# Two transformer blocks in one launch: another order of work between block 1's experts and block 2's attention

## The chip, the cores and the metric

The kernel runs on one core of a Trainium2 chip. The metric is device time in microseconds (us): the time of the program from start to end on that core, as the median of several runs. Five engines work side by side, each through its own list of instructions, in the order in which they stand in that list: TensorE (PE in the profile, its weight loads PEld), VectorE (DVE), ScalarE (ACT), GpSimd (POOL) and SyncE (SP, which here only starts transfers). An instruction that waits for another engine holds up everything behind it on its own engine.

## The reference

Two blocks run one after the other on 256 tokens of width 1024. Block 1 is attention with convolution, and then a mixture of 32 experts; block 2 is a gated pooling and attention block with a feed-forward layer. What matters here is the seam between them:

```python
# end of block 1
h = h + rms_norm(ffn, post_ffn_norm)          # ffn: routed experts + shared expert
# start of block 2
u = rms_norm_2(h, norm_mix)
proj = u @ w_in                                # pooling, q, k, v and two gates
z_pool, q, k, v, g_pool, g_attn = jnp.split(proj, splits, axis=-1)
y_pool = multiscale_pool(z_pool, w_pool_group, pool_scale) @ w_pool_branch
y_attn = windowed_gqa(q, k, v, sink) @ w_attn_branch
merged = jax.nn.sigmoid(g_pool) * y_pool + jax.nn.sigmoid(g_attn) * y_attn
h = h + merged @ w_out
```

`multiscale_pool` takes, for each of four groups of 128 channels, a centred mean over 2, 4, 8 or 16 tokens minus the token, and multiplies it by a 128x128 matrix of its group. `windowed_gqa` is attention with 8 query heads over 2 key heads.

## The kernel before

The 256 tokens are two tiles of 128, tile 0 and tile 1. Each fp32 operand of a large product is split in a high part (rounded to the type that TensorE takes at full rate) and a low part (the rest): ScalarE casts the high part, VectorE subtracts to get the low one. A product is then three matmuls, high by high, high by low, low by high (`mm3`, lines 278, 279 and 280). Weights stream in through `W`: SyncE starts the loads, `W.take()` hands out the next granule, `W.ahead()` splits granules in advance (lines 122 and 125).

The work around the change stands in this order in the code:

1. The experts' results are brought back to token order by one-hot matmuls (`scatter`, line 1143) and the shared expert is added (`shared_last`, line 1136), into PSUM tiles `ffn[i][n]`, i the token tile, n the half of 512 columns. Tile 1's part of it is spread around tile 0's next steps.
2. `residual(i, ...)` closes block 1 for tile i: ScalarE squares the two halves of `ffn[i]` (line 204), VectorE multiplies them by the gain into `mg` (`gained`, line 319), works out the inverse root in eight short instructions (lines 247, 222, 224 and 251; the profile shows three of them merged), adds to the residual stream `h` (line 251) and multiplies by the next gain (line 338). For the second half of a tile in `late` the gain product comes after the first half's line 338.
3. `half_T` (line 258) transposes four 128x128 blocks of `mg` into a PSUM tile `tr`. From it `split` (lines 76 and 77) writes the high part `uTh` on ScalarE and the low part `uTl` on VectorE.
4. `u_cols("q2", i, ...)` makes the queries of tile i: eight steps k of three matmuls, 24 in all, into the PSUM tile `q`. Steps 0 to 3 read the first half of `uTh` and `uTl`, steps 4 to 7 the second half.
5. Then come the keys and values (`kv`), and four times `pool_in(g)` (24 matmuls into `zp`, then sums over tokens on VectorE that end in `res`) and `pool_group(g, res)` (line 1379, a matmul of `res` into `pg`, an instruction on VectorE at line 1381, a split). Between them stand `scores2(i, j)` (line 1322: two PSUM tiles `s2a` and `s2b`, which VectorE reads at line 251 into `pr`) and `softmax2(i)`.

A scheduler sets the order on each engine. It takes the order of the code as the base and `tc.issue_after(x)` as an added condition that an instruction stands behind x. PSUM tiles come from two pools of four buffers each: `mm` (`tr`, `q`, `kv`, `zp`, `gt`, and `ffn[1]`) and `acc` (`s2a`, `s2b`, `pg`, `q2T`, `pT2`, `av2`). A pool hands its buffers out in turn, and a tile can be written only when the readers of the last tile in its buffer are done.

Of the kernel before, what the change touches and what calls it, by code (L numbers as in the profile page):

```python
# [11 lines left out]
F32 = mybir.dt.float32  # L12
# [8 lines left out]
P = 128  # L21
# [39 lines left out]
def block_kernel(ctx, tc, rwt, x, meta, pos, wst, gains, cst, pvec, rbias, sink, wpg, cst2, out):  # L61
    nc = tc.nc
    PE, ACT, DVE, POOL = nc.tensor, nc.scalar, nc.vector, nc.gpsimd
# [153 lines left out]
    last = [None] * 3  # L217
# [35 lines left out]
    def half_T(src, b, p=P):  # L253

        pt = mmt("tr")
        v = pt[:, :4 * p].rearrange("q (a t) -> q a t", a=4)
        for a in range(4):
            PE.transpose(v[:, a], src[:, (4 * b + a) * P:(4 * b + a + 1) * P], ident[:p, :p])
        return v

    def transpose_split(src, hi, lo, p, c0, n=8, pts=None):

        for b, v in enumerate(pts or [half_T(src, b, p) for b in range(n // 4)]):
            ins = split(v, hi[:, 4 * b:4 * b + 4, c0:c0 + p], lo[:, 4 * b:4 * b + 4, c0:c0 + p])
        return ins
# [57 lines left out]
    def residual(i, parts, g, g_next, s2, c=None, c32=1 / 32, late=(0,)):  # L323


        s = sm(2)
        mg = w4("mg")
        for n, a in enumerate(parts):
            sl = slice(n * 512, n * 512 + 512)
            last[0] = square(a, s[:, n:n + 1], c32)  # L330
            if n == 0 or i not in late:
                gained(mg[:, sl], a, c, g[:, sl])
        r = rstd(s)
        for n in range(2):
            sl = slice(n * 512, n * 512 + 512)
            with tc.issue_after(ins.ins) if n else nullcontext():
                stt(h[:, i, sl], mg[:, sl], r, h[:, i, sl], ALU.mult, ALU.add)
            last[1] = ins = DVE.tensor_mul(mg[:, sl], h[:, i, sl], g_next[:, sl])
            if i in late and n == 0:
                with tc.issue_after(ins.ins):  # L340
                    gained(mg[:, 512:], parts[1], c, g[:, 512:])
        return mg
# [33 lines left out]
    with tc.tile_pool(name="p1", bufs=1) as p1:  # L376
# [465 lines left out]
        ws = [W.take() for _ in range(4)]  # L842
# [4 lines left out]
        s2 = sm(4)  # L847
# [4 lines left out]
        nx = []  # L852
# [12 lines left out]
    with tc.tile_pool(name="p2", bufs=1) as p2:  # L865
# [76 lines left out]
        for c in (0, S):  # L942
            for i in range(2):
                oh_ins = DVE.tensor_scalar(oh[:, i, c:c + S], cs[:, C_IOTA + c:C_IOTA + c + S], code[:, i:i + 1],
                                           None, op0=ALU.is_equal)
# [11 lines left out]
        ws = [W.take() for _ in range(4)]  # L957
# [171 lines left out]
        ffn = [[acct("ffn00"), acct("ffn01")], None]  # L1129
# [9 lines left out]
        def scatter(i, gs):  # L1139
            for g in gs:  # L1140
                for n in range(2):
                    for a in range(2):
                        PE.matmul(ffn[i][n], sel[:, g, i * P:(i + 1) * P],
                                  ys[g][:, a * D + n * 512:a * D + (n + 1) * 512], start=False,
                                  stop=g == 3 and a == 1, skip_group_check=True)

        g_pf = gain("post_ffn")
        g_m2 = gain("mix2")
# [67 lines left out]
                        DVE.tensor_copy(raw, pa)  # L1216
                        DVE.tensor_add(ffn[i][n], ffn[i][n], raw)
        s2 = sm(4)
        nx = [residual(0, ffn[0], g_pf, g_m2, s2)]
        scatter(1, (0, 2))  # L1220
        shared_last(1, (1,))
        W.drop(WHOLE[2])
        pts = [half_T(nx[0], 0)]
        scatter(1, (1,))
        pts.append(half_T(nx[0], 1))
        scatter(1, (3,))
    pg.close()


    with tc.tile_pool(name="p3", bufs=1) as p3:  # L1230
        uTh = p3.tile([P, 8, S], F32R, name="uTh", tag="th")
        uTl = p3.tile([P, 8, S], F32R, name="uTl", tag="tl")
        with tc.tile_pool(name="p3a", bufs=1) as q3:
# [22 lines left out]

            rn, dgs = [], []

            def u_cols(name, i, ws, n):

                o = mmt(name)[:, :n]
                c = G // n
                for k in range(8):
                    w = ws[k // c]
                    mm3(o, [(uTh[:, k, i * P:(i + 1) * P], uTl[:, k, i * P:(i + 1) * P],
                             kb(w[0], k % c, n), kb(w[1], k % c, n))], k == 0, k == 7)
                return o
# [15 lines left out]
                ACT.copy(kT[:, i * P:(i + 1) * P], o)  # L1283

            o_q = []
            transpose_split(nx[0], uTh, uTl, P, 0, pts=pts)
            ws = [W.take() for _ in range(4)]
            o_q.append(u_cols("q2", 0, ws, 512))
            nx.append(residual(1, ffn[1], g_pf, g_m2, s2))
            with tc.issue_after(last[0].ins):  # L1290
                h_squares(0, s2)
            rn.append(rstd(s2[:, 0:2]))
# [11 lines left out]
            ws = [W.take() for _ in range(2)]  # L1304
# [13 lines left out]
            def scores2(i, j):  # L1318
                o = [acct("s2a"), acct("s2b")]
                for a in range(2):  # L1320
                    for b in range(2):
                        PE.matmul(o[b][:, a * S:(a + 1) * S],
                                  qT[b * 64:(b + 1) * 64, j + a, i * P:(i + 1) * P],
                                  kT[b * 64:(b + 1) * 64], start=True, stop=True, skip_group_check=True)
                for b in range(2):
                    for a in range(2):
                        hd = b * 4 + j + a
                        stt(pr[i][:, hd], c2[:, 64 + i * 256:320 + i * 256], 2.0 ** -(hd + 1),
                            o[b][:, a * S:(a + 1) * S], ALU.mult, ALU.add)
                    DVE.tensor_reduce(mxs[i][:, b * 4 + j:b * 4 + j + 2], pr[i][:, b * 4 + j:b * 4 + j + 2],  # L1330
                                      axis=AX.X, op=ALU.max)

            def softmax2(i):
                mx = mxs[i]
                DVE.tensor_tensor(mx, mx, skb, op=ALU.max)
                nm = sm(8)
                DVE.tensor_scalar(nm, mx, -1.0, None, op0=ALU.mult)
                es = sm(8)
                DVE.tensor_tensor(es, skb, nm, op=ALU.add)
                ACT.activation(es, es, AF.Exp)  # L1340
                for hd in range(NH):
                    ACT.activation(pr[i][:, hd], pr[i][:, hd], AF.Exp, bias=nm[:, hd:hd + 1],
                                   accum_out=sus[i][:, hd:hd + 1])
                return es
# [32 lines left out]
            def pool_group(g, res):  # L1377
                o = acct("pg")[:, :S]
                PE.matmul(o, kb(wpt, g), res, start=True, stop=True)
                y = pw("yp")[:, :S]  # L1380
                DVE.tensor_scalar(y, o, pv_[:, V_PSC + g:V_PSC + g + 1], None, op0=ALU.mult)
                split(y, yph[:, g], ypl[:, g])
# [61 lines left out]
            res = [pool_in(0)]  # L1444
            scores2(0, 0)
            scores2(0, 2)
            es0 = softmax2(0)
            pool_group(0, res[0])
            res.append(pool_in(1))
            scores2(1, 0)  # L1450
            scores2(1, 2)
            es1 = softmax2(1)
            pool_group(1, res[1])
            res.append(pool_in(2))
            denom(0, es0)
            pTx = [q3.tile([P, 2, 512], F32, name="pTa", **kw) for kw in ({}, {"tag": "q4"})]
            pTb = [[t[:, c] for t in pTx for c in range(2)], 0]
# [40 lines left out]
            ws = [W.take() for _ in range(4)]  # L1498
            s2 = sm(4)
            out_last(o2, gh, gl, ws, 0)  # L1500
            W.ahead(1)
            nx = [normed(0, o2[0], g_f2, s2)]
# [11 lines left out]
        with tc.tile_pool(name="p3b", bufs=1) as q3:  # L1514
# [55 lines left out]
            ws = [W.take() for _ in range(4)]  # L1570
# [25 lines left out]
            ws = [W.take() for _ in range(4)]  # L1596
            for d in range(4):
                down(18 + d, ws[d], 0)
            s2 = sm(4)
# [194 lines left out]
```

## Time and profile before

| | |
|---|---|
| median of 3 runs | 789.06 us (788.62 to 791.53) |
| the profiled execution: its own time | 790.79 us |
| the profiled execution: span from first to last instruction | 788.8 us |
| TensorE busy | 766.5 us, 97% of the span |
| VectorE busy | 611.8 us, 78% |
| ScalarE busy | 468.7 us, 59% |
| mean granted TensorE clock | 0.992 of full speed |

The profile is one execution. Its times below are counted from the start of the span. Busy TensorE is a model for the ends of matmuls, so starts are read rather than ends. The place of the change lies at about 440 to 500 us.

### The profile page before, as it was taken

Reading aid. Unit: us, or ns where it says so; the run is one execution under the profiler, and the core shown is the slowest. Engines: PE = TensorE matmul, PEld = TensorE weight load, DVE = VectorE, ACT = ScalarE, POOL = GpSimd, SP = SyncE. Lnnn points to the kernel's source line nnn. Section 1 sums busy time; section 2 is a strip of 40 time slices with the busy share of each in tenths; the row PEclk is TensorE's granted clock in tenths of the full one; section 3 lists DMA queues with packets and bytes.
Section 4 is the critical chain, followed back from the end, with each engine's and each line's share of the span. In section 5 each row is a group of like instructions: output and inputs, shape, how many; then the busy total and the mean of one; then the engine's idle time right before and its main releaser. Section 6 shows DMA issues by size and latency. Waiting matters only on the chain. (4 is left out here: it accounts for less than half of the span.)

```text
span 788.8 us, 11966 instructions
## 1 busy us (share of the span) xinstructions
PE 766.5 (97%) x4579; PEld 665.4 (84%) x4579; DVE 611.8 (78%) x987; ACT 468.7 (59%) x697; POOL 45.7 (6%) x62
## 2 busy tenths in 40 slices
PE   7989999999999999999999899999999999999996
PEld 5979985788888888888877688999988999999995
DVE  5878678799999989998988879766868566566565
ACT  5656445488887878887776466434555444444442
POOL 5641200000000000000000100000000000000000
PEclk9989999999999999999999999999999999999999
DMA  8737354589898979998998751444445545555101
GB/s 338 306 108 248 108 214 160 215 332 369 317 359 317 371 287 370 370 369 312 371 355 307 262 186 56 161 160 163 165 163 208 199 173 197 178 188 186 54 1 54
DMA packets 27212, 182.48 MB, mean 231 GB/s; under 512 B 3328, under 2 KB 3584, under 8 KB 6160
## 3 DMA queue, kind: packets, MB, share of 16 engines
q1 hardware_dynamic: 25344, 176.96, 60.5%
q0 software_dynamic: 1056, 3.71, 1.4%
q10 hardware_dynamic: 752, 1.01, 0.4%
q8 instruction: 37, 0.61, 0.3%
q14 instruction: 23, 0.19, 0.1%
HBM read 180.62 MB, written 1.05 MB: 230 GB/s over the span
## 5 line engine op out<-in xcount | busy, mean ns | idle before, releaser
L125 DVE TENSOR_TENSOR wlo<-raw,whi 128x1024 fp32r<-128x1024 f32 x324 | 391.4, 1225 | 84.7 <-ACT whi L122 77.5
L122 ACT CAST whi<-raw 128x1024 fp32r<-128x1024 f32 x326 | 337.6, 1049 | 176.0 <-PE gu L279 49.1
L278 PE MATMUL gu<-whi,xg 128*128 128x512 f32 x256 | 102.8, 401 | 0.0
L279 PE MATMUL gu<-wlo,xg 128*128 128x512 f32 x256 | 101.3, 396 | 0.0
L280 PE MATMUL gu<-whi,xg 128*128 128x512 f32 x256 | 100.6, 393 | 0.0
L279 PE MATMUL gu<-u2l,whi 128*128 128x256 f32 x320 | 90.6, 283 | 0.0
L278 PE MATMUL gu<-u2h,whi 128*128 128x256 f32 x320 | 90.6, 283 | 0.0
L280 PE MATMUL gu<-u2h,wlo 128*128 128x256 f32 x320 | 90.5, 283 | 0.0
L279 PEld LDWEIGHTS gu<-u2l,whi 128*128 128x128 f32 x320 | 61.5, 192 | 0.0
L280 PEld LDWEIGHTS gu<-u2h,wlo 128*128 128x128 f32 x320 | 61.4, 192 | 0.0
L278 PEld LDWEIGHTS gu<-u2h,whi 128*128 128x128 f32 x320 | 61.4, 192 | 0.0
L279 PEld LDWEIGHTS gu<-wlo,xg 128*128 128x128 f32 x256 | 48.2, 188 | 11.1 <-DVE wlo L125 1.4
L280 PEld LDWEIGHTS gu<-whi,xg 128*128 128x128 f32 x256 | 48.1, 188 | 10.5
L278 PEld LDWEIGHTS gu<-whi,xg 128*128 128x128 f32 x256 | 48.1, 188 | 9.9
L280 PE MATMUL y<-whi,hl 128*128 128x512 f32 x128 | 50.5, 394 | 0.0
L279 PE MATMUL y<-wlo,hh 128*128 128x512 f32 x128 | 50.5, 394 | 0.0
L278 PE MATMUL y<-whi,hh 128*128 128x512 f32 x128 | 49.1, 400 | 0.0
L278 PE MATMUL f<-whi,sh 128*128 128x512 f32 (+1 forms) x110 | 38.2, 349 | 0.0
L279 PE MATMUL f<-wlo,sh 128*128 128x512 f32 (+1 forms) x110 | 38.1, 349 | 0.0
L280 PE MATMUL f<-whi,sl 128*128 128x512 f32 (+1 forms) x110 | 37.7, 347 | 0.0
L278 PE MATMUL gt<-uTh,whi 128*128 128x256 f32 x128 | 36.7, 287 | 0.0
L280 PE MATMUL gt<-uTh,wlo 128*128 128x256 f32 x128 | 36.3, 283 | 0.0
(457 smaller groups left out, 1480.8 us busy)
## 6 DMA issues: line engine op xcount, KB each, us to landing
raw<-in_wst_dram SPq DMA_DIRECT2D x164, 1024.0 KB, 4.8
gain<-in_gains_dram POOLq DMA_DIRECT2D x6, 512.0 KB, 4.4
raw<-in_wst_dram SPq DMA_DIRECT2D x5, 512.0 KB, 8.1
h<-in_x_dram SPq DMA_DIRECT2D x2, 512.0 KB, 4.8
cs<-in_cst_dram SPq DMA_DIRECT2D x1, 612.0 KB, 16.6
out_dram<-mg ACTq DMA_DIRECT2D x2, 256.0 KB, 2.8
out_dram<-mg SPq DMA_DIRECT2D x2, 256.0 KB, 2.6
c<-in_cst_dram POOLq DMA_DIRECT2D x1, 288.0 KB, 3.1
```

The lines of the kernel that those rows point to most:

```text
L122: ACT.copy(hi, src)
L125: eng.tensor_sub(lo, src, hi.bitcast(F32))
L278: PE.matmul(o, sh, mh, start=first and i == 0, stop=False, skip_group_check=True)
L279: PE.matmul(o, sh, ml, start=False, stop=False, skip_group_check=True)
L280: last_mm[0] = PE.matmul(o, sl, mh, start=False, stop=last and i == n - 1, skip_group_check=True)
```

## The change

Four things are changed in the code. First, in `residual(0, ...)` no half is late: both gain products of tile 0 stand ahead of the inverse root. Second, the low half of tile 0's first four transposed blocks must stand behind the last product of that residual (`mul_ins`), and the last four blocks are no longer transposed ahead of the queries but between steps 3 and 4 of tile 0's query product, with their split there. Third, `residual(1, ...)` stands behind the second high half of tile 0 (`hi_ins`), and both its halves are late. Fourth, `pool_group(0)` moves behind the scores of tile 1, and `pool_group(1)` behind `pool_in(2)`.

```diff
--- before.py
+++ after.py
@@ -1216,14 +1216,13 @@
                         DVE.tensor_copy(raw, pa)
                         DVE.tensor_add(ffn[i][n], ffn[i][n], raw)
         s2 = sm(4)
-        nx = [residual(0, ffn[0], g_pf, g_m2, s2)]
+        nx = [residual(0, ffn[0], g_pf, g_m2, s2, late=())]
+        mul_ins = last[1]
         scatter(1, (0, 2))
         shared_last(1, (1,))
         W.drop(WHOLE[2])
         pts = [half_T(nx[0], 0)]
-        scatter(1, (1,))
-        pts.append(half_T(nx[0], 1))
-        scatter(1, (3,))
+        scatter(1, (1, 3))
     pg.close()
 
 
@@ -1256,11 +1255,13 @@
 
             rn, dgs = [], []
 
-            def u_cols(name, i, ws, n):
+            def u_cols(name, i, ws, n, done=None):
 
                 o = mmt(name)[:, :n]
                 c = G // n
                 for k in range(8):
+                    if done:
+                        done(k)
                     w = ws[k // c]
                     mm3(o, [(uTh[:, k, i * P:(i + 1) * P], uTl[:, k, i * P:(i + 1) * P],
                              kb(w[0], k % c, n), kb(w[1], k % c, n))], k == 0, k == 7)
@@ -1283,10 +1284,19 @@
                 ACT.copy(kT[:, i * P:(i + 1) * P], o)
 
             o_q = []
-            transpose_split(nx[0], uTh, uTl, P, 0, pts=pts)
+            def first_cols(k):
+
+                if k % 4 == 0:
+                    v = pts[0] if k == 0 else half_T(nx[0], 1)
+                    hi_ins[0] = ACT.copy(uTh[:, k:k + 4, :P], v)
+                    with tc.issue_after(mul_ins.ins):
+                        DVE.tensor_sub(uTl[:, k:k + 4, :P], v, uTh[:, k:k + 4, :P].bitcast(F32))
+
+            hi_ins = [None]
             ws = [W.take() for _ in range(4)]
-            o_q.append(u_cols("q2", 0, ws, 512))
-            nx.append(residual(1, ffn[1], g_pf, g_m2, s2))
+            o_q.append(u_cols("q2", 0, ws, 512, first_cols))
+            with tc.issue_after(hi_ins[0].ins):
+                nx.append(residual(1, ffn[1], g_pf, g_m2, s2, late=(0, 1)))
             with tc.issue_after(last[0].ins):
                 h_squares(0, s2)
             rn.append(rstd(s2[:, 0:2]))
@@ -1445,13 +1455,13 @@
             scores2(0, 0)
             scores2(0, 2)
             es0 = softmax2(0)
-            pool_group(0, res[0])
             res.append(pool_in(1))
             scores2(1, 0)
             scores2(1, 2)
+            pool_group(0, res[0])
             es1 = softmax2(1)
+            res.append(pool_in(2))
             pool_group(1, res[1])
-            res.append(pool_in(2))
             denom(0, es0)
             pTx = [q3.tile([P, 2, 512], F32, name="pTa", **kw) for kw in ({}, {"tag": "q4"})]
             pTb = [[t[:, c] for t in pTx for c in range(2)], 0]
```

What this makes of each engine's list is shown at three places. The first is TensorE where the experts' scatter ends and the queries of block 2 begin (`ffn_4318` is the second half of tile 1, `tr` a PSUM tile of transposed blocks, `q` the query tile of token tile 0). Before:

```order
L1143 MATMUL ffn_4318<-yg_4319,sel 128x512
L258 MATMUL tr<-ident,mg 128x128 x4
L1143 MATMUL ffn_4318<-yg_4319,sel 128x512
L258 MATMUL tr<-ident,mg 128x128 x4
L278 MATMUL q_4566<-whi,uTh 128x512
```

After:

```order
L1143 MATMUL ffn_4318<-yg_4319,sel 128x512 x2
L258 MATMUL tr<-ident,mg 128x128 x4
L278 MATMUL q_4557<-whi,uTh 128x512
L279 MATMUL q_4557<-wlo,uTh 128x512
L280 MATMUL q_4557<-whi,uTl 128x512
```

The second four transposes have left this place: they stand behind the twelfth query matmul now, and twelve more follow them.

The second place is VectorE's list behind the inverse root of tile 0 (`ffn_4317` and `ffn_4318` are the two halves of tile 1, `sm` a short instruction of tile 1's inverse root). Before:

```order
L251 SCALAR_TENSOR_TENSOR h<-mg,sm_4505,h 128x512
L77 TENSOR_TENSOR uTl<-tr,uTh 128x4x128
L338 TENSOR_TENSOR mg<-h,gain 128x512
L319 TENSOR_TENSOR mg<-ffn_4317,gain 128x512
L319 TENSOR_TENSOR mg<-ffn_4318,gain 128x512
L77 TENSOR_TENSOR uTl<-tr,uTh 128x4x128
L247 SCALAR_TENSOR_TENSOR sm_4599<-sm_4591 128x1
```

After:

```order
L251 SCALAR_TENSOR_TENSOR h<-mg,sm_4506,h 128x512
L338 TENSOR_TENSOR mg<-h,gain 128x512
L1293 TENSOR_TENSOR uTl<-tr,uTh 128x4x128 x2
L319 TENSOR_TENSOR mg<-ffn_4317,gain 128x512
L247 SCALAR_TENSOR_TENSOR sm_4598<-sm_4591 128x1
```

Tile 0's last product (line 338) stands ahead of both low halves now, and everything of tile 1's residual stands behind the second low half. The gain product of `ffn_4318` has moved further back, behind tile 1's first line 338.

The third place is TensorE at the scores of tile 1 and the first pooling product (`zp_4914` and `zp_4908` are the pooling input of group 1, `zp_4997` of group 2; `res_4861` is the result of group 0). Before, the product stood among the matmuls of group 1:

```order
L278 MATMUL zp_4914<-uTh_4547,whi_4716 128x256
L279 MATMUL zp_4914<-uTl_4548,whi_4716 128x256
L1379 MATMUL pg_4905<-res_4861,wpt_4556 128x256
L280 MATMUL zp_4914<-uTh_4547,wlo_4717 128x256
L278 MATMUL zp_4914<-uTh_4547,whi_4716 128x256
```

After, it stands among those of group 2, behind the scores of tile 1:

```order
L1332 MATMUL s2a_4962<-kT2_4553,qT2_4555 128x256
L1332 MATMUL s2b_4963<-kT2_4553,qT2_4555 128x256
L278 MATMUL zp_4997<-uTh_4542,whi_4742 128x256
L279 MATMUL zp_4997<-uTl_4543,whi_4742 128x256
L280 MATMUL zp_4997<-uTh_4542,wlo_4743 128x256
L278 MATMUL zp_4997<-uTh_4542,whi_4742 128x256
L279 MATMUL zp_4997<-uTl_4543,whi_4742 128x256
L1389 MATMUL pg_4974<-res_4861,wpt_4551 128x256
```

The scores of tile 1 now follow those of tile 0 with 24 matmuls and no pooling product between them, so their four PSUM tiles take the four `acc` buffers that the scores of tile 0 held, in the same turn, and `pg_4974` takes the next one. The second pooling product has moved by 19 matmuls behind the first, to the end of group 2.

## Rows read from the trace of the kernel before

**Rows 1.** Waits of TensorE, 436 to 530 us: total us, times, longest us.

```profile
PE tr L258 <- DVE mg L338: 1.9, 1, 1.9
PE pg L1379 <- DVE res L1374: 1.8, 2, 1.3
```

**Rows 2.** Timeline of TensorE: start, us, instruction, idle before and its releaser.

```profile
445.19 0.60 PE L258 MATMUL tr<-ident,mg 128*128 128x128 f32 x4
...
447.88 0.63 PE L258 MATMUL tr<-ident,mg 128*128 128x128 f32 x4 [1.85 <-DVE mg L338]
448.26 0.48 PE L278 MATMUL q<-whi,uTh 128*128 128x512 f32 x1
...
453.82 1.04 PE L258 MATMUL tr<-ident,mg 128*128 128x128 f32 x8
455.20 0.49 PE L373 MATMUL rs<-dg,ones 128*128 128x128 f32 x2 [0.34 <-DVE dg L367]
455.44 0.48 PE L278 MATMUL q<-whi,uTh 128*128 128x512 f32 x1
```

**Rows 3.** Timeline of VectorE at the two residuals.

```profile
443.03 0.69 DVE L338 TENSOR_TENSOR mg<-h,gain 128x512 f32<-128x512 f32 x1
443.64 0.68 DVE L319 TENSOR_TENSOR mg<-ffn,gain 128x512 f32<-128x512 f32 x1
444.36 0.75 DVE L251 SCALAR_TENSOR_TENSOR h<-mg,sm,h 128x512 f32<-128x512 f32 x1
446.44 0.69 DVE L77 TENSOR_TENSOR uTl<-tr,uTh 128x512 fp32r<-128x512 f32 x1 [1.33 <-ACT uTh L76]
447.05 0.68 DVE L338 TENSOR_TENSOR mg<-h,gain 128x512 f32<-128x512 f32 x1
...
449.77 0.15 DVE L247 SCALAR_TENSOR_TENSOR sm<-sm 128x1 f32<-128x1 f32 x1
...
451.23 0.75 DVE L251 SCALAR_TENSOR_TENSOR h<-mg,sm,h 128x512 f32<-128x512 f32 x1
...
452.02 0.69 DVE L338 TENSOR_TENSOR mg<-h,gain 128x512 f32<-128x512 f32 x1
```

**Rows 4.** Timeline of ScalarE at tile 0's first high half.

```profile
445.82 0.59 ACT L76 CAST uTh<-tr 128x512 fp32r<-128x512 f32 x1
446.31 0.60 ACT L204 ACTIVATE junk<-ffn 128x512 bf16<-128x512 f32 x1
...
447.03 0.63 ACT L204 ACTIVATE junk<-h 128x512 bf16<-128x512 f32 x1
```

**Rows 5.** Timeline of TensorE at the pooling products and the scores of tile 1.

```profile
475.11 0.70 PE L1379 MATMUL pg<-res,wpt 128*128 128x256 f32 x2 [1.28 <-DVE res L1374]
475.46 0.47 PE L280 MATMUL zp<-uTh,wlo 128*128 128x256 f32 x1
...
478.37 0.48 PE L1322 MATMUL s2a<-kT,qT 64*128 64x256 f32 x1
...
480.33 0.38 PE L278 MATMUL zp<-uTh,whi 128*128 128x256 f32 x1
...
484.09 0.70 PE L1379 MATMUL pg<-res,wpt 128*128 128x256 f32 x2 [0.51 <-DVE res L1374]
```

**Rows 6.** Timeline of VectorE: last read of tile 0's scores, second of tile 1's.

```profile
478.41 0.41 DVE L251 SCALAR_TENSOR_TENSOR pr<-c,s2b 128x256 f32<-128x256 f32 x1
...
481.38 0.41 DVE L251 SCALAR_TENSOR_TENSOR pr<-c,s2a 128x256 f32<-128x256 f32 x1
```

**Rows 7.** Stretches: us, busy us (instructions) of each engine, granted clock, DMA.

```profile
45.00:50.00 5.00, 3.75 (x18) 3.74 (x18) 2.92 (x6) 2.74 (x4) 2.94 (x2) 0.54 0.63 210
50.00:55.00 5.00, 5.00 (x32) 4.90 (x31) 2.94 (x11) 2.31 (x5) 0.29 (x1) 0.78 0.01 2
...
446.00:448.00 2.00, 0.15 (x2) 0.15 (x2) 1.56 (x3) 1.94 (x6) 1.33 (x3) 1.00 0.96 384
...
476.00:486.00 10.00, 9.49 (x77) 8.65 (x76) 10.00 (x31) 7.52 (x22) 0.14 (x2) 1.00 0.19 80
```

## Prediction

> **What bounds the kernel now.** First I read the table of busy shares: TensorE is close to always busy, so time is lost or won where it waits. Next, its list of waits over the whole stretch that the change touches. It has two rows of size [rows 1]: a transpose that waits 1.9 us for tile 0's `mg`, and two pooling products that wait 1.8 us for `res`. A third, 0.3 us, is the idle of the `rs` row in [rows 2]. Nothing else up to 530 us holds TensorE, so I take a shift at 485 us as carried to the end. If all of this vanished and nothing replaced it, 4 us would be won; that is the ceiling.
>
> Then the timelines, engine by engine, to see who is late. TensorE does the first transposes at 445.19, then idles 1.85 us until 447.88 [rows 2]. The second half of `mg` is late because VectorE stood still: it idled 1.33 us for the high half `uTh`, then did `uTl`, and only then the product `mg` at 447.05 [rows 3], whose inputs were there at about 445.1 (`h` began at 444.36 and takes 0.75). VectorE works in list order. This is what the change repairs, and also, I think, what it builds anew one step later.
>
> **The front, step by step**, in the clock of the trace of before. The first transposes slip by one scatter matmul, 0.23 us (24 queries and what starts them take 453.82 - 448.26 = 5.56 us, [rows 2]), to 445.42. They take 0.63 [rows 2], the cast 0.59 [rows 4]; with 0.03 and 0.06 for the hand-overs the queries start at 446.7. `mg` is no longer an obstacle: the first half began at 443.03 [rows 3], now about 0.6 later because a second gain product (0.61 apart, 443.03 to 443.64) stands ahead of it, and the second half follows at about 445.0. Query matmul 3 needs the low half: 446.1 + 0.59 + 0.03 + 0.69 [rows 3] + 0.06 = 447.45. Nine more at 0.23, and the second transposes stand at 449.7.
>
> Here the price comes. VectorE's next instruction is the second low half, which needs these transposes and their cast. Until then, from 447.4 to 451.0, VectorE stands still, with the whole residual of tile 1 behind it; ScalarE's squares of tile 1 also stand behind that cast. TensorE idles about 0.9 us for each of the two casts.
> - Cast: 449.7 + 0.63 + 0.03 = 450.4. Squares: 0.49 to the first, 0.72 more to the second, 0.72 for that one (446.31 and 447.03, [rows 4]): the inverse root starts at 452.3. Before it started at 449.77 [rows 3].
> - Root to `h` 1.46 (449.77 to 451.23), `h` to product 0.79 (451.23 to 452.02): the first half of `mg` starts at 454.6. Before, 452.02.
> - Now the gain product of `ffn_4318`, 0.61 later, `h` 0.72 after it (443.64 to 444.36), product 0.79 later: second half at 456.7, finished 0.69 later and handed over at 457.45. Four transposes take 0.38 (447.88 to 448.26), and the queries of tile 1 start at 457.8.
>
> Before, they started at 455.44 [rows 2]: the front is 2.4 us later there. TensorE's own work would have been done at 454.0 (twelve matmuls from 451.0, with 0.2 for a low half), which hardly differs from 453.82. What costs is the wait for tile 1: about 1.3 us ahead of its first four transposes and 1.7 ahead of the second four. Before, the whole residual of tile 1 lay under the queries of tile 0; that cover is gone for 3 us of it.
>
> One piece of the front moves: the first `rs` matmul (0.24, 455.20 to 455.44) stands behind tile 1's queries now, so it is paid later: +0.24. The second `rs` needs the diagonal of tile 1's root, which hangs on the last casts; these move by 3.2 us (eight transposes from 453.82, the second four 0.38 behind, against 457.45), the queries by 2.4. I put 0.2 for that wait, between 0 and 0.8. Front: 2.4 + 0.24 + 0.2 = **+2.8 us**. Bounds: +1.8 (each of the some 15 hand-overs 0.05 shorter, no `rs` wait) to +3.6.
>
> **The back.** Removed are the two pooling waits, 1.28 + 0.51 = 1.8 us [rows 5]. Both have one cause, VectorE, which is busy for all of the 10 us from 476 to 486 [rows 7] while it makes `res` and reads the scores. So I ask what TensorE needs next from it. Without the wait and the product (0.35, 475.11 to 475.46) it comes to the scores of tile 1 at some 476.6 instead of 478.37 [rows 5]. They take 1.96 (478.37 to 480.33), half of it for each pair of PSUM tiles. The last of the four `acc` buffers, though, is read at 478.41 for 0.41 us [rows 6], in a list whose order up to there is unchanged. So the last pair, due at 477.6, waits until 478.9: 1.3 us, and group 2 begins at 479.85. Five `zp` matmuls on (0.13 each: 22 in the 2.91 us from 475.46 to 478.37) stands the first pooling product, at 480.5. Its `acc` buffer is that of tile 1's first `s2a`, whose second read VectorE did at 481.38 [rows 6], now some 0.4 earlier as the 0.4 us instruction behind `pg` has left: done at 481.4. That is 0.9 us more. The second product then begins at 481.4 + 0.35 + 19 x 0.125 = 484.1, where it began at 484.09 [rows 5], and finds its buffer and `res` ready; one `zp` matmul (0.13) that stood ahead of it is still to do. So what is taken out comes back: **+0.1**. Bounds: -1.8 (the buffers are free after all) and +0.8 (VectorE's list is longer ahead of the last read by the two parts of a split, 0.35 each).
>
> The first edit, an early gain product of tile 0, costs 0.6 us on VectorE, covered by the scatter that TensorE does until 445.4. Without that cover it would be 0.6 us on the path. No transfer changes its place: the lists of SP and POOL keep their order.
>
> Sum: 2.8 + 0.1 = **+2.9 us**. Against the profiled execution's own 790.79 us that is 793.7. That execution lies 1.7 us above the median of the runs shown; against the median, which I forecast, 789.06 + 2.9 = **792.0 us**, 0.37% slower. A difference of 0.5%, 3.9 us, is about what a measurement of this kernel tells from none.
>
> **Rivals.**
> 1. *The clock falls* (slower, the other side). In this trace the granted clock was 0.54 in the mean from 45 to 50 us, where TensorE stood idle for 1.25 us, and 0.78 from 50 to 55 [rows 7]: 5 x 0.46 + 5 x 0.22 = 3.4 us of full clock lost, or some 6.8 us at the half level, 1.2 GHz. The idle at 446 to 448 us did not lower it (1.00, [rows 7]). The new gap, 454.0 to 457.45, has 3 us of idle with four small transposes in the middle; this rival decides if that counts as one idle stretch. At half clock a 512-column query takes twice as long: of those 6.8 us TensorE worked in 5.6, which cost 2.8 us; half such a stretch costs 1.4. I take 2.1: 794.1 us. The Trainium skill (TensorE: Matmul & The Clock Gate, Part 1) says that half clock is the default, which activity lifts and an idle stretch brings back. By that rule the sum would be +5.0 us, not +2.9. The trace agrees at 45 us and shows no fall at 447 us.
> 2. *Tile 1 stays hidden*: VectorE comes to tile 1's residual early enough that the first `mg` half of tile 1 is done by 454.0. Then the front costs nothing, and with the back between 0 and -1.8 the time is 787.2 to 789.1, say 788.5. Against it stands VectorE's list, where the second low half precedes all of tile 1.
> 3. *All waits vanish*: front and back each lose theirs, 1.9 + 0.3 + 1.8 = 4.0 us: 785.1. For it speaks only that each has been moved behind other work.
>
> **How the numbers follow.** Forecast (+1.2 to +4) 0.52; clock 0.33; tile 1 hidden 0.11; all waits vanish 0.04. The range leaves out 0.1 at each end: 789.0 reaches into the second rival, 796.0 over the first with its full 2.8 us (794.7) and the runs' own spread of 2.9 us. The likeliest case alone gives 790.3 to 793.1. Chances: faster by over 0.5% 0.05 (rival 3 and a bit of 2); slower by over 0.5%, that is over 793.0, 0.37 (rival 1 and the upper edge of the forecast); within 0.58.
>
> **What the profile after would show.** VectorE idle for about 3.5 us ahead of tile 0's second low half; TensorE with some 0.9 us ahead of each half's queries, 1.3 and 1.7 us ahead of tile 1's transposes, and tile 1's queries 12.4 us after the first transposes (before 10.25). In the scores of tile 1 a wait for `pr`, ahead of `pg` one of under 1 us. Wrong would be: `mg` of tile 1 ready before TensorE asks for it; no wait at the scores; the granted clock below 1 between 454 and 465 us (rival 1).

## The result, and the profile after

The changed kernel took 794.65 us in the median of 5 runs (791.95 to 797.04), beside 790.5 us for the kernel before: the ratio is 1.0066, with a 95% interval of 1.0043 to 1.0088, 5.2 us slower. Timed again beside other kernels on another occasion (a2 below) it was 1.0051 (1.0031 to 1.0071), 4.0 us slower. These ratios are not quotients of the medians, which lie 4.2 and 3.5 us apart; the differences in us given for the runs below are the ratio's. Predicted were 792.0 us, +2.9 us, in a range of 789.0 to 796.0. The profiled execution took 792.67 us, span 790.9 us, mean granted clock 0.991.

The waits of TensorE over the stretch that the change touches, after (waited-for, total us, times, longest); they answer to [rows 1]:

```profile
PE tr L258 <- DVE mg L338: 2.5, 2, 1.4
PE q L278 <- ACT uTh L1291: 1.3, 2, 0.7
PE pg L1389 <- DVE pr L251: 0.6, 1, 0.6
PE s2b L1332 <- DVE pr L251: 0.6, 1, 0.6
```

The one wait for tile 0's `mg` is gone, and so are both for `res`. In their place stand two for tile 1's `mg`, two for the casts and two for `pr`. The timeline of TensorE, after, for [rows 2]:

```profile
443.25 0.60 PE L258 MATMUL tr<-ident,mg 128*128 128x128 f32 x4
444.53 0.50 PE L278 MATMUL q<-whi,uTh 128*128 128x512 f32 x1 [0.67 <-ACT uTh L1291]
...
447.66 0.60 PE L258 MATMUL tr<-ident,mg 128*128 128x128 f32 x4
448.94 0.50 PE L278 MATMUL q<-whi,uTh 128*128 128x512 f32 x1 [0.68 <-ACT uTh L1291]
...
449.66 0.50 PE L280 MATMUL q<-whi,uTl 128*128 128x512 f32 x1
...
453.33 0.63 PE L258 MATMUL tr<-ident,mg 128*128 128x128 f32 x4 [1.09 <-DVE mg L338]
455.36 0.78 PE L258 MATMUL tr<-ident,mg 128*128 128x128 f32 x4 [1.40 <-DVE mg L338]
455.79 0.78 PE L278 MATMUL q<-whi,uTh 128*128 128x512 f32 x1
```

And that of VectorE, after, for [rows 3]:

```profile
442.85 0.69 DVE L338 TENSOR_TENSOR mg<-h,gain 128x512 f32<-128x512 f32 x1
444.51 0.69 DVE L1293 TENSOR_TENSOR uTl<-tr,uTh 128x512 fp32r<-128x512 f32 x1 [0.96 <-ACT uTh L1291]
448.92 0.69 DVE L1293 TENSOR_TENSOR uTl<-tr,uTh 128x512 fp32r<-128x512 f32 x1 [3.72 <-ACT uTh L1291]
449.52 0.68 DVE L319 TENSOR_TENSOR mg<-ffn,gain 128x512 f32<-128x512 f32 x1
450.23 0.16 DVE L247 SCALAR_TENSOR_TENSOR sm<-sm 128x1 f32<-128x1 f32 x1
...
452.49 0.69 DVE L338 TENSOR_TENSOR mg<-h,gain 128x512 f32<-128x512 f32 x1
...
454.62 0.68 DVE L338 TENSOR_TENSOR mg<-h,gain 128x512 f32<-128x512 f32 x1
```

VectorE stands still for 3.72 us ahead of the second low half, and everything of tile 1's residual begins behind it. Tile 1's queries start at 455.79 - 443.25 = 12.54 us after tile 0's first transposes; before it was 10.25.

The granted clock (the number behind the five engines) in stretches of 2 us, after:

```profile
452.00:454.00 2.00, 0.86 (x6) 0.42 (x4) 2.00 (x7) 0.01 (x1) 0.00 (x0) 1.00 0.01 4
454.00:456.00 2.00, 0.64 (x5) 0.65 (x6) 2.00 (x6) 0.58 (x1) 0.94 (x2) 0.94 0.28 102
456.00:458.00 2.00, 2.00 (x6) 1.59 (x6) 1.30 (x5) 1.82 (x5) 0.28 (x3) 0.50 0.97 301
458.00:460.00 2.00, 2.00 (x8) 1.56 (x7) 1.26 (x8) 1.62 (x3) 0.00 (x0) 0.71 0.32 121
```

From 456 to 458 it is at its lower level, 1.2 GHz. The kernel was profiled once more in a2, and there the same two waits, 1.09 and 1.40 us, stand at 453.75 and 455.78, but the clock stayed up:

```profile
454.00:456.00 2.00, 0.60 (x6) 0.36 (x5) 2.00 (x8) 0.59 (x1) 0.54 (x1) 1.00 0.12 23
456.00:458.00 2.00, 2.00 (x12) 1.69 (x11) 1.72 (x6) 1.53 (x4) 0.69 (x3) 1.00 0.84 303
458.00:460.00 2.00, 2.00 (x11) 1.63 (x10) 0.96 (x7) 2.00 (x5) 0.00 (x0) 1.00 0.53 207
```

Executions differ ahead of the place of the change too (the clock falls for a time between 45 and 55 us, by different amounts): mark A below, ahead of which the change alters only the residual of tile 0, lies anywhere from 439.01 to 442.70. So spans are not compared whole. Three marks in TensorE's timeline cut the rest of a span: A, the start of the last four matmuls of line 1136; B, the first score of tile 0; C, the second pooling product.

| kernel | A | B | C | span | A to B | B to C | C to end | A to end, against before |
|---|---|---|---|---|---|---|---|---|
| before | 441.84 | 471.41 | 484.09 | 788.8 | 29.57 | 12.68 | 304.71 | 0 |
| after | 439.67 | 473.41 | 486.20 | 790.9 | 33.74 | 12.79 | 304.70 | +4.27 |
| a2 (after again) | 440.09 | 472.56 | 485.35 | 790.0 | 32.47 | 12.79 | 304.65 | +2.95 |
| e1 front alone | 439.87 | 472.33 | 485.01 | 789.7 | 32.46 | 12.68 | 304.69 | +2.87 |
| e2 back alone | 439.06 | 468.63 | 481.42 | 786.1 | 29.57 | 12.79 | 304.68 | +0.08 |
| e3 keep busy | 442.70 | 475.16 | 487.96 | 792.7 | 32.46 | 12.80 | 304.74 | +3.04 |
| e9 all gaps | 439.87 | 472.31 | 485.10 | 789.8 | 32.44 | 12.79 | 304.70 | +2.97 |
| e5 residual first | 439.90 | 470.21 | 483.01 | 787.7 | 30.31 | 12.80 | 304.69 | +0.84 |
| e4 both ahead | 442.68 | 471.42 | 484.10 | 788.8 | 28.74 | 12.68 | 304.70 | -0.84 |
| e6 scatter between | 441.64 | 470.02 | 482.70 | 787.4 | 28.38 | 12.68 | 304.70 | -1.20 |
| e7 other buffers | 439.01 | 468.58 | 480.13 | 785.8 | 29.57 | 11.55 | 305.67 | -0.17 |
| e8 low half moved | 439.75 | 468.14 | 480.83 | 785.5 | 28.39 | 12.69 | 304.67 | -1.21 |
| e10 low between | 440.13 | 469.04 | 481.73 | 786.4 | 28.91 | 12.69 | 304.67 | -0.69 |
| e11 low half, 2 | 439.32 | 467.69 | 482.91 | 787.9 | 28.37 | 15.22 | 304.99 | +1.62 |

A to B holds the front, B to C the back. With the clock up, the parts agree to 0.1 us between kernels that share them, which makes the table finer than the timed ratios, whose intervals are some 1.1 to 1.8 us to either side. The table has one execution of each kernel, though, and it leaves out what lies ahead of A.

### The profile page after: what moved, and what is told of

It is laid out like the page before. It is cut to its first block, busy times and chain, and to the rows that moved or that the text cites. A ratio compares the mean times of both kernels' runs of the same rounds, so it can differ in the third digit from the quotient of the medians.

```text
span 790.9 us, 11967 instructions
## 1 busy us (share of the span) xinstructions
PE 768.2 (97%) x4579; PEld 665.7 (84%) x4579; DVE 611.8 (77%) x987; ACT 469.0 (59%) x697; POOL 45.5 (6%) x62
```

## The experiments

**e1 and e2: each half alone.** e1 is the changed kernel with the pooling products where they stood before; e2 is the kernel before with only this:

```diff
-            pool_group(0, res[0])
             res.append(pool_in(1))
             scores2(1, 0)
             scores2(1, 2)
+            pool_group(0, res[0])
             es1 = softmax2(1)
+            res.append(pool_in(2))
             pool_group(1, res[1])
-            res.append(pool_in(2))
```

Expected of e1:

> The front of the change alone (residuals, low halves and transposes as changed), the pooling products where they stood before. Theory (VectorE's list: the second low half of tile 0 stands ahead of tile 1's residual, and the gap that this opens on TensorE lets the clock fall): nearly the whole loss is here, 3.5 to 5 us over the kernel before, tile 1's queries again about 12.5 us after the first transposes (before 10.25), two waits for mg ahead of tile 1's transposes of 1.0 to 1.7 us, the granted clock below 1 within the 4 us behind them. Rival (the loss comes from the moved pooling products): within 1 us of the kernel before.

Measured: ratio 1.0043 (1.0027 to 1.0060), +3.4 us, just under what was expected; waits ahead of tile 1's transposes 1.10 and 1.40 us; but the granted clock behind them is 1.00. Expected of e2:

> The back of the change alone (pooling products of groups 0 and 1 issued later), the front as before. Theory: what is taken out comes back, 0.1 us more, between -1.8 and +0.8, so the same as before by any measurement; from the scores of tile 0 to the second pooling product 12.8 us as against 12.68. Rival (the loss of the change sits here): 2 us or more over the kernel before.

Measured: 0.9998 (0.9981 to 1.0014), B to C 12.79. The loss is in the front. Of the theory's two parts the list order stands; the clock did not fall in this execution, with the same waits, where a fall was expected.

**e3 and e9: TensorE kept busy in the gaps.** e3 puts matmuls of existing operands, into columns of PSUM that nobody reads, ahead of tile 1's transposes; e9 also in both waits for a cast:

```diff
+            keep_busy(8)
+            pts1 = [half_T1(0)]
+            keep_busy(10)
+            pts1.append(half_T1(1))
-            ins = transpose_split(nx[1], uTh, uTl, P, P)
+            ins = transpose_split(nx[1], uTh, uTl, P, P, pts=pts1)
```

> The changed kernel with 18 added matmuls of 256 columns whose results nobody reads, 8 ahead of tile 1's first four transposes and 10 ahead of the second four, where TensorE waited 1.09 and 1.40 us. Theory: the waits stay, since VectorE is late by itself, but the clock does not fall: granted clock 1.00 from 454 to 460 us, tile 1's queries spaced by 0.23 us from the first on, still about 12.5 us after tile 0's first transposes; 1.2 us less than the changed kernel, 4 us over the kernel before. Rival A (the clock falls for another reason than the gap, or the gap was not what lowered it): the same granted clock as in the changed kernel and the same time. Rival B (the fall costs more in other executions than in the one profiled): 2 us or more less than the changed kernel.

> The changed kernel with 28 added matmuls of 256 columns whose results nobody reads: 5 in each of the two waits of 0.68 us for tile 0's casts, 8 and 10 ahead of tile 1's transposes. Theory (beside 2.95 us of waits and moved work, which the trace shows in every execution, the changed kernel loses clock in the gap in many executions): the work is again 2.9 to 3.1 us longer than before, up to 0.2 us more where an added matmul is late, and the excess over before falls to 2 to 3 us, from 4 to 5 us, with some executions at a mean granted clock of 0.994 or above, as the kernel before has them in half of its executions and the changed kernel in none of 11. Rival (the clock in the executions of the changed kernel is low by chance, or for a cause elsewhere): 4 to 5 us over the kernel before again, no execution at 0.994.

Measured: e3 1.0026 (1.0010 to 1.0042), +2.1 us; e9 1.0033 (1.0017 to 1.0050), +2.6 us. In both the waits ahead of tile 1's transposes are filled, tile 1's queries come no earlier (455.95 - 443.44 = 12.51 us after the first transposes in e9), and the clock is 1.00 behind them. In the timeline of TensorE in e9 the second four transposes still wait for VectorE:

```profile
452.28 1.11 PE L1293 MATMUL rs<-whi 128*128 128x256 f32 x8
453.51 0.63 PE L1320 MATMUL tr<-ident,mg 128*128 128x128 f32 x4
453.89 1.43 PE L1293 MATMUL rs<-whi 128*128 128x256 f32 x10
455.54 0.66 PE L1320 MATMUL tr<-ident,mg 128*128 128x128 f32 x4 [0.21 <-DVE mg L338]
455.95 0.47 PE L278 MATMUL q<-whi,uTh 128*128 128x512 f32 x1
```

So what costs is that VectorE is late, whatever TensorE does meanwhile. The timed excess over before is 2.1 and 2.6 us, less than the 4.0 and 5.2 of the changed kernel, as the theory of the clock has it, though also less than the 3.04 and 2.97 of their own rows in the table. And 2 of 12 and 3 of 11 executions reach a mean granted clock of 0.994, which none of the changed kernel's 11 did (a2 below included). The intervals overlap, though, and e6 and e8 below, which have no such gap, reach it in only 2 of 12 each: that the clock behind the gap is the rest of the excess is not shown.

**a2: the changed kernel again.** 

> The changed kernel once more, on the same chip as the three others of this group, to set its size beside them. Theory (waits of 2.4 to 2.8 us in every execution, and a fall of the clock behind them in some of them): 3 to 5 us over the kernel before, and the lower the mean granted clock of an execution the longer it takes. Rival (the front alone, 3.4 us, is already all of it, and the first five runs lay high by chance): the same as the front alone within 1 us. Rival (the two halves of the change disturb each other): 5 us or more again, with waits that neither half shows alone.

Measured: 1.0051 (1.0031 to 1.0071), 792.32 us in the median of 6; A to end +2.95. Its executions go by the clock: 791.81 to 791.85 us at 0.993, 792.8 us at 0.991, 794.1 us at 0.990, 794.6 us at 0.989. The halves do not disturb each other: A to B is that of e1, B to C that of e2. The 4.0 us are within 1 us of e1's 3.4, so the first rival, that the first five runs lay high by chance, is not excluded.

**e5: tile 1's residual ahead of the second low half**, with both its gain products early (`late=()`), the second transposes of tile 0 staying in the middle of the queries (the edit is cut to what matters here):

```diff
+                if k == 4:
+                    with tc.issue_after(hi_ins[0].ins):
+                        nx.append(residual(1, ffn[1], g_pf, g_m2, s2, late=()))
                 if k % 4 == 0:
...
-            with tc.issue_after(hi_ins[0].ins):
-                nx.append(residual(1, ffn[1], g_pf, g_m2, s2, late=(0, 1)))
```

> The changed kernel with one difference: tile 1's residual stands ahead of tile 0's second high and low half on ScalarE and VectorE (both gain products of tile 1 early); the second four transposes of tile 0 stay in the middle of the query product. Theory (the loss comes from VectorE's list, in which the second low half stands ahead of all of tile 1's residual): no waits ahead of tile 1's transposes, a wait of about 1 us for the second low half in the queries instead, tile 1's queries 10.0 to 10.7 us after the first transposes (changed 12.5, before 10.25), 2 to 3.5 us less than the changed kernel. Rival (it is the transposes in the middle of the queries that cost, wherever the residual stands): tile 1's queries 12 us or more after the first transposes, the same time as the changed kernel.

Measured: 1.0017 (1.0003 to 1.0032), +1.3 us; A to B 30.31, which is 2.16 us less than in a2; tile 1's queries come 10.22 us after the first transposes, where 10.0 to 10.7 was expected. The timeline of TensorE in e5, at the second half of tile 0's queries and at both transposes of tile 1, which wait for nothing now (its first four, at 449.74, now stand among tile 0's queries):

```profile
449.17 0.50 PE L278 MATMUL q<-whi,uTh 128*128 128x512 f32 x1 [0.68 <-ACT uTh L1295]
...
449.74 0.60 PE L258 MATMUL tr<-ident,mg 128*128 128x128 f32 x4
450.92 0.50 PE L280 MATMUL q<-whi,uTl 128*128 128x512 f32 x1 [0.58 <-DVE uTl L1297]
...
453.35 0.60 PE L258 MATMUL tr<-ident,mg 128*128 128x128 f32 x4
```

The waits for `mg` are gone, one of 0.58 us for the low half has come, where about 1 us was expected. Most of the front's loss was VectorE's list. What is left of it, 0.74 us, goes with the waits inside the query product: two of 0.68 us for the casts and the one for the low half.

**e4 and e6: only the early second half.** e4 keeps the early gain product and puts both transposes ahead of the queries:

```diff
-        scatter(1, (1, 3))
+        scatter(1, (1,))
+        pts.append(half_T(nx[0], 1))
+        scatter(1, (3,))
...
-                    v = pts[0] if k == 0 else half_T(nx[0], 1)
+                    v = pts[k // 4]
...
-                nx.append(residual(1, ffn[1], g_pf, g_m2, s2, late=(0, 1)))
+                nx.append(residual(1, ffn[1], g_pf, g_m2, s2))
```

> One piece of the front only: tile 0 has both gain products early and both low halves behind its last product, as in the change, but both halves are transposed ahead of the query product, and tile 1's residual stands behind the second high half with one late half, as before; pooling products as before. Theory (what made TensorE wait 1.85 us was that VectorE waited for a cast between tile 0's two halves, and what the change built anew was tile 0's second low half waiting for transposes in the middle of the queries): both waits are gone, tile 1's queries about 8.3 us after the first transposes (before 10.25, changed 12.54), 1.5 to 2 us less than before. Rival (VectorE cannot have tile 1's residual ready any earlier, so the wait moves ahead of tile 1's transposes whatever the order): tile 1's queries 10 us or more after the first transposes, the same time as before.

e6 is e4 with four scatter matmuls made to follow the first transposes:

```diff
+        scatter(1, (1,))
         pts = [half_T(nx[0], 0)]
-        scatter(1, (1,))
+        with tc.issue_after(last_tr[0].ins):
+            scatter(1, (3,))
         pts.append(half_T(nx[0], 1))
-        scatter(1, (3,))
```

> As the kernel with both transposes ahead of the queries, with the last four scatter matmuls put between tile 0's first and second four transposes, so that they cover the first cast. Theory (what is left of the front is the 0.95 us that TensorE waits for cast and low half): the wait shrinks to 0.3 to 0.6 us and up to 0.6 us of it comes back ahead of tile 1's second four transposes, since VectorE's residual of tile 1 ends only some 0.35 us earlier; 0.3 to 1 us less than with both ahead, about 2 us less than before. Rival (VectorE is the bound there already): the wait moves in full to tile 1's transposes, the same as with both ahead.

Measured: e4 0.9981 (0.9966 to 0.9997), 1.5 us faster than before; e6 0.9988 (0.9972 to 1.0004). The timeline of TensorE in e4:

```profile
446.25 1.05 PE L258 MATMUL tr<-ident,mg 128*128 128x128 f32 x8
448.26 0.50 PE L278 MATMUL q<-whi,uTh 128*128 128x512 f32 x1 [0.95 <-DVE uTl L1295]
...
453.81 1.15 PE L258 MATMUL tr<-ident,mg 128*128 128x128 f32 x8
455.09 0.50 PE L278 MATMUL q<-whi,uTh 128*128 128x512 f32 x1
```

Tile 1's queries come 455.09 - 446.25 = 8.84 us after the first transposes, where 8.3 was expected: one wait of 0.95 us is left, and the table's gain, 0.84 us, is below the 1.5 to 2 that was expected. In e6 that one is gone too, and the rest of [rows 1] now stands ahead of tile 1:

```profile
PE pg L1392 <- DVE res L1387: 1.8, 2, 1.3
PE tr L258 <- DVE mg L338: 0.7, 1, 0.7
PE rs L373 <- DVE dg L367: 0.2, 1, 0.2
```

By the table the front of e6 is 1.2 us shorter than before, 4.1 us shorter than a2's; against e4 that is 0.36 us, which the timed ratios cannot tell.

**e7: other buffers in the back.** e2 with one line more:

```diff
-                o = [acct("s2a"), acct("s2b")]
+                o = [mmt("s2a"), mmt("s2b")] if (i, j) == (1, 2) else [acct("s2a"), acct("s2b")]
```

> The back of the change alone, with the last pair of score tiles of tile 1 in the PSUM pool mm in place of acc. Theory (the waits that the later pooling products bring are for acc buffers): the waits for pr at the last scores of tile 1 and at the first pooling product go (0.6 us each on TensorE's list, 0.5 to 1 us each on that of its weight loads), TensorE then meets res of group 1 about 1.2 us before VectorE has it, so the second pooling product comes 11.5 us after the scores of tile 0 (12.8 with the back alone) and the time falls by about 1.2 us. Rival (VectorE, busy for 10 us on end, bounds the stretch however the buffers lie): the waits only change their name, the second pooling product again 12.5 us or more after the scores, the same time.

The timeline of TensorE in e2, at the waits for the buffers, and then in e7:

```profile
476.10 0.48 PE L1322 MATMUL s2b<-kT,qT 64*128 64x256 f32 x1 [0.56 <-DVE pr L251]
...
478.61 0.70 PE L1379 MATMUL pg<-res,wpt 128*128 128x256 f32 x2 [0.60 <-DVE pr L251]
...
481.42 0.59 PE L1379 MATMUL pg<-res,wpt 128*128 128x256 f32 x2
```

```profile
475.49 0.70 PE L1379 MATMUL pg<-res,wpt 128*128 128x256 f32 x2
480.13 0.70 PE L1379 MATMUL pg<-res,wpt 128*128 128x256 f32 x2 [1.07 <-DVE res L1374]
...
489.29 0.67 PE L1379 MATMUL pg<-res,wpt 128*128 128x256 f32 x2 [0.61 <-DVE res L1374]
```

The waits were for `acc` buffers: in other buffers they are gone, and the second product comes 480.13 - 468.58 = 11.55 us after the scores, as expected. But the expected 1.2 us is not won: 1.0 us is given back behind C (305.67 beside e2's 304.68), 0.61 of it in a wait for the third `res`. The timed ratio is 1.0014 (1.0001 to 1.0028), +1.1 us, where the table has -0.17. Buffers made the waits; without them VectorE's `res` is what TensorE waits for next.

**e8 and e11: a low half on GpSimd.** Both are e6 with one argument more, `W.ahead(eng=POOL if g == 0 else None)` in `pool_in` for e8, `g == 1` for e11.

> As the kernel with scatter matmuls between the two transposes, and the one 1024-column low half of a weight granule that VectorE makes inside the first pooling input (1.2 us, ahead of res of group 0) is made by GpSimd, which stands idle there. Theory (in the stretch of the pooling products VectorE is the bound, the score buffers are only where it is met): VectorE has res of group 0 about 1.2 us earlier, the waits of the pooling products for res shrink from 1.8 us to 0.3 or less, and 1.2 to 1.8 us are won beside the front's 1.2: about 3 us less than before. Rival A (as with the score tiles in the other pool, what is won there is paid back a few us later): waits of the same sum in the 20 us behind, the time of the kernel with the scatter matmuls between. Rival B (the low half on GpSimd, at 2.4 us, comes late for its matmuls): a wait for wlo on TensorE.

> As the kernel with scatter matmuls between the two transposes, and the low half of a weight granule that stands on VectorE directly ahead of res of group 0 (1.23 us; the one moved earlier was another one, which stood in idle time of VectorE) is made by GpSimd. Theory (VectorE bounds the stretch of the pooling products): the first pooling product no longer waits 1.28 us; another low half has moved up in VectorE's list ahead of res of group 1, so the second product waits 0.5 to 1.7 us; from the scores of tile 0 to the second pooling product 11.4 to 12.7 us (12.68), 0 to 1.3 us less in all. Rival (score buffers or TensorE's own order bound the stretch): the first wait vanishes and the second product comes at 12.7 us again, with waits of another name.

e8 measured 0.9979 (0.9964 to 0.9995), 1.7 us faster than before, but by the table it is e6: its low half was one that VectorE made in idle time, so that it tells nothing of the theory. e11 took the right one and measured 1.0018 (1.0004 to 1.0033); the first product waits 2.38 us, more than before. The timeline of VectorE and of GpSimd in e11:

```profile
468.81 0.42 DVE L251 SCALAR_TENSOR_TENSOR res<-ws,zp 128x256 f32<-128x256 f32 x1
469.15 0.41 DVE L251 SCALAR_TENSOR_TENSOR pr<-c,s2a 128x256 f32<-128x256 f32 x1
469.48 2.05 DVE L1386 TENSOR_TENSOR res<-ws,c 128x8 f32<-128x8 f32 x2
471.45 0.41 DVE L251 SCALAR_TENSOR_TENSOR pr<-c,s2a 128x256 f32<-128x256 f32 x1
```

```profile
468.87 2.56 POOL L125 TENSOR_TENSOR wlo<-raw,whi 128x1024 fp32r<-128x1024 f32 x1 [17.03 <-PE s2b L1335]
```

Two instructions on 8 columns, 0.23 us in e6, take 2.05 us, until GpSimd's low half is done. The 1.23 us taken off VectorE came back as 1.8, and behind the 2.38 us the clock fell (last section), which is part of the 15.22 us from B to C. Neither theory foresaw it, and whether VectorE alone bounds the back is not settled by it.

**e10: the second low half behind tile 1's first gain product**, on top of e8:

```diff
+            low0 = low(0, mul_ins)
+            with tc.issue_after(his[1].ins), tc.issue_after(low0.ins):
+                nx.append(residual(1, ffn[1], g_pf, g_m2, s2, hook=lambda x: low(4, x)))
```

> As the kernel with the low half on GpSimd, and tile 0's second low half on VectorE behind tile 1's first gain product (it waited for its cast before; the product was ready). Theory (VectorE's list is what makes tile 1's second transposes late by 0.68 us): that wait falls to 0.1 to 0.4 us, 0.3 to 0.6 us less than the kernel with the low half on GpSimd. Rival (the cast, not the list, sets when tile 1's inverse root can start): the same wait of 0.6 to 0.7 us, the same time.

Measured: 0.9986 (0.9970 to 1.0002); by the table 0.52 us slower than e8; ahead of tile 1's transposes stand waits of 0.27 and 0.83 us in place of one of 0.7. The theory fell: the gain product was not ready. In VectorE's timeline it waits for ScalarE's square of the same PSUM tile, with the low half behind it:

```profile
446.01 0.69 DVE L319 TENSOR_TENSOR mg<-ffn,gain 128x512 f32<-128x512 f32 x1 [1.28 <-ACT junk L204]
446.62 0.68 DVE L1296 TENSOR_TENSOR uTl<-tr,uTh 128x512 fp32r<-128x512 f32 x1
```

## Why the prediction was right, and what it mis-sized

**The front, +2.8.** Right: A to B is 32.47 - 29.57 = 2.90 us longer in a2 and 2.89 in e1. Counted from the first transposes, in the profile after: the queries at 1.28 us (predicted 1.28), query matmul 3 at 2.00 (2.03), the second transposes at 4.41 (4.28), the inverse root at 6.98 (6.88), the first half of `mg` at 9.24 (9.18), tile 1's queries at 12.54 (12.38). VectorE's idle time, predicted some 3.5 us, is 3.72. The mechanism is shown by its undoing: e5 puts tile 1's residual, its second gain product included, ahead of that low half, and both waits for `mg` are gone.

**The waits ahead of tile 1** are 1.09 and 1.40 us where 1.3 and 1.7 were named, and ahead of each cast 0.67, where 0.9 was: the busy time of the matmuls and transposes ahead of each gap reaches further into it than was counted. The starts are right to 0.2 us. The 0.2 us for the second `rs` is not there in the profile after; its bound of 0 was the value.

**The back, +0.1.** Right in size, +0.11 in a2 and e2, and place by place. From the first score of tile 0, the wait of the last scores ends at 7.48 us (predicted 478.9, that is 7.49), the first pooling product comes at 9.99 us (predicted 481.4, that is 9.99). e7 shows that these were waits for buffers, and also that the bound of -1.8 for free buffers was not to be had: without the waits VectorE's `res` is the next thing late.

**The early gain product, nothing.** Right, and more than that: together with both transposes ahead of the queries (e4) it is the useful part of the change.

**The clock, rival 1.** Not taken into the sum. Its sign, a granted clock below 1 between 454 and 465 us, is there in the profile after. Of the three profiled executions with the unfilled gap (after, a2, e1) it fell in one; there it cost 33.74 - 32.47 = 1.27 us, close to the 1.4 that the rival gives for half of its stretch: TensorE was at half clock for some 3.4 us in all (2 x 0.06 + 2 x 0.50 + 2 x 0.29 = 1.7 us of full clock lost in the rows above), half of the 6.8 us seen at 45 us. The Trainium skill (TensorE: Matmul & The Clock Gate, Part 1) says of the rise of the clock under steady matmuls that its moment differs from run to run. The traces here show something like it for the fall: behind equal waits it came in one execution (0.50) and not in two others (1.00).

**The time.** The median of 794.65 us lies 2.65 above the forecast of 792.0: 1.44 of it is the kernel before, which took 790.5 where the forecast set out from 789.06, and 1.25 the change. The forecast of +2.9 is what the work behind A costs, 2.95; the timed +5.2 and +4.0 lie 2.3 and 1.1 us above that. A fall of the clock in the gap is one cause seen. It is not the only one: a2's profiled execution has no fall there and is still 3.9 us longer than e2's (790.0 and 786.1), 1.0 us of it ahead of A, where the clock fell by different amounts between 40 and 55 us. And timed ratios scatter about the table: e7's lies 1.3 us above its row without any such gap, e3's 0.9 below. How the rest divides between these stays open, and so does how often the clock falls in executions without a profile.

**Rivals 2 and 3.** Out: VectorE did not come to tile 1 in time, and each wait that was taken out had a successor.

## What to carry to other kernels

On an engine that works in list order, an instruction moved later must not drag unrelated work behind it: the second low half itself was needed at 449.66 us, but the whole residual of tile 1 stood behind its wait. Before a wait is taken out, ask which queue its resource comes from and who is busy there; in the back both the buffers and `res` hung on VectorE, so that 1.8 us of waits only changed name. Keep the part of a change that pays: the early gain product, with both transposes ahead of the queries, is faster than both kernels: by 0.2% of the kernel before in e4 and e8, with intervals that end just below 1, while e6's reaches 1.0004; by the table 0.8 to 1.2 us.

## What the runs showed of the hardware

Whether the clock falls behind a wait of TensorE is not the same in every execution: behind 1.09 and 1.40 us with four transposes between, it fell once in three profiles; behind one of 1.85 us in [rows 2] it did not; and behind the 2.38 us in e11 it did, as these stretches of e11 show (in stretches of 2 us it is 0.61 from 472 to 474 and 0.54 from 474 to 476):

```profile
470.00:480.00 10.00, 7.93 (x50) 7.22 (x51) 9.05 (x23) 2.84 (x4) 1.51 (x3) 0.83 0.29 107
480.00:490.00 10.00, 9.01 (x76) 8.75 (x75) 10.00 (x32) 8.34 (x28) 0.28 (x4) 1.00 0.00 0
```

And GpSimd beside a busy VectorE is not free: beside a 2.56 us subtraction on GpSimd two 8-column VectorE instructions took 1.8 us longer than in e6, all of it the first one (1.98 us in the trace), while the one just ahead of them, which reads the scores from PSUM, took its usual 0.41 beside the same subtraction. The Trainium skill (SBUF — State Buffer, SBUF: two separate sides) says that a VectorE instruction with two inputs from SBUF and a GpSimd instruction that reads SBUF share a pair of ports, which the one that starts first holds for its whole instruction. The rows of e11 agree, though no run here isolated it.
